# A hybrid decoder layer: weights of twelve projection units split early and kept in DRAM as two parts

## The chip, the cores and the metric

The kernel runs on one core of one Trainium2 chip. Its time is the device time of one execution in microseconds (us). TensorE (PE) does the matmuls, VectorE (DVE), ScalarE (ACT) and GpSimd (POOL) the rest, and SyncE (SP) issues nearly all DMAs. Each engine works through its own queue in order; semaphores order the engines among each other.

## What is computed

One layer over x of 1024 positions by 1024 columns. The reference, cut to what matters here:

```python
u = rms_norm(h, attn_norm[layer])
proj = jnp.einsum('bsd,dc->bsc', u, w_in[layer])
(dq, dk, dv, sq, ckv, iq, ik, iw, rq, rk, rv, gate) = jnp.split(proj, split_points, axis=-1)
o_a = diff_attention(dq, dk, dv, ...)            # two softmaxes a head, their difference times v
o_b = dsa_attention(sq, rms_norm(ckv), iq, ik, iw, ...)  # index scores, top 256 keys a query, attention
o_c = retention(rotary(rq), rotary(rk), rv, ...)
y = jax.nn.silu(gate) * concat(o_a, o_b, o_c)
h = h + jnp.einsum('bsc,cd->bsd', y, w_out[layer])
return rms_norm(h, final_norm)
```

## The kernel before

**Units.** The input projection is cut into units of 128 columns (256 for rq, rk, rv): iq0 to iq3 make the index queries, q0 to q2 and k0 to k2 the queries and keys of the differential attention, s0 to s2 and ck those of the sparse attention, g0 to g7 the gate. `gemm` runs a unit. Every product of two float32 operands is made of three matmuls over two-part numbers: uh and ul are the parts of u, wh and wl those of a weight. In the trace lines 130, 131 and 132 are the products wh x uh, wh x ul and wl x uh of a 128-column unit, and lines 347 to 349 those of a 256-column unit.

**The split.** `wsplit` loads a unit's weights in two halves of 256 KB into wr (two buffers, SP issues), and for each half POOL writes wh (L119, a rounding copy, 128x512) and wl (L123, the rest, 128x512). wh and wl live in tag w, five buffers of 4 KB a partition, so that two units fit and one tile of a third: wl of a unit can be written when the unit before the last one has ended on PE.

**Order.** `run` writes the program in stages: the front (v, index keys), iq0, iq1; then the index scores (`idx_scores`, lines 408 and 409 on PE, 411 on ACT, 416 on DVE) interleaved with iq2, iq3, q0, k0; then the differential attention (`diff`: scores L718, softmax L729 on DVE and L731 on ACT, POOL's scaling pq at L744, the combination L747 on DVE, transposes L678, product with v L693) beside the top-k bisection (`topk`, L443 to L464 on DVE, L457 on ACT, with one copy hb, L431, on POOL) and the remaining units; then the sparse attention, retention and the output. PE's queue has exactly the order in which the program is written. On the other engines a scheduler decides when the program is built: it takes, by its own estimate of time, whatever is ready and comes first in the program.

**Around the split.** POOL also splits some evicted results (hl, L119 and L366), rotates (rt), and finishes norms (f, L510 to L531). `mix` interleaves several streams by their costs and weights.

Of the kernel before, what the change touches and what calls it, by code (L numbers as in the profile page):

```python
# [10 lines left out]
F = mybir.dt.float32  # L11
FR = mybir.dt.float32r
# [9 lines left out]
KC = 8  # L22
# [5 lines left out]
C_DQ, C_DK, C_DV, C_SQ, C_CKV, C_IQ, C_IK, C_RQ, C_RK, C_RV, C_G = (  # L28
    0, 384, 768, 1152, 1536, 1664, 2176, 2248, 2504, 2760, 3016)
WA = 384 + 72  # L30
C_R = (C_RQ, C_RK, C_RV)
K = {'mk': 'up ky', 'mp': 's2 g5 g4', 'rt': ('hl', 'pq'), 's0': ('gg', 'ag', 'gg', 'ag', 'gg', 'ag', 'gg', 'ag'), 'xp': 2, 'bufs': (8, 3, 3, 5, 3, 4, 1), 'pp': (7,), 'rot': 0, 'order': 'g0 g1 k1 q1 k2', 'order2': 'q2 g2 rq g6 s0 ck g7 s1 M g3 rv rk | ', 'wd': 36, 'wt': 13, 'wg': 119, 'gw': 56, 'rw': 26, 'rx': 132, 'pw': 40, 'ow': 84, 'nf': 2, 'ev': 200, 'late': 8, 'de': ('aa', 'aa', 'aa'), 'da': 'ax', 'gd': (7, 4, 2), 'hlp': 'sqkk', 'tkp': '', 'vt': 'v', 'rs': 'x', 'nv': 1, 'dn': 'v', 'ws': 'gg', 'oe': ('av', 'gg'), 'one': 0, 'idx': (42, 40), 'iqs': 'iq2 iq3 q0 k0'}
NST, NP, NPQ, NW, NHL, NHALF, NY = K["bufs"]


# [10 lines left out]
def mix(*streams):  # L46
    live = [[g, float(total), 0.0] for g, total in streams]
    while live:
        s = min(live, key=lambda v: v[2] / v[1])
        try:  # L50
            c = next(s[0])
            s[2] += c
            yield c
        except StopIteration:
            live.remove(s)


def interleave(*streams):
    for _ in mix(*streams):
        pass  # L60


def drain(*gens):
    for g in gens:
        for _ in g:
            pass


class Trunk:
    def __init__(self, ctx, tc, ins, out):  # L70
        self.tc, self.nc = tc, tc.nc
        self.i, self.out = ins, out
        self.sb = ctx.enter_context(tc.tile_pool(name="sb", bufs=1))
        self.ps = ctx.enter_context(tc.tile_pool(name="ps", bufs=1, space=PSUM))
        self.dr = ctx.enter_context(tc.tile_pool(name="dr", bufs=1, space=bass.MemoryType.DRAM))
        self.n = 0
        self.late = []
        self.qd, self.gd, self.rt = {}, {}, {}
        self.yo = {c: self.dram(f"yo{c}", [128, S]) for c in (0, 1, 2)}
        self.gr = self.dram("gr", [2, 128, S])  # L80
        self.gd[6], self.gd[7] = self.gr[0], self.gr[1]
        self.yd = [self.dram(f"yd{j}", [8, 128, 512]) for j in range(2)]
# [225 lines left out]
    def wsplit(self, c0, w):  # L308
        hs, ls = [], []
        if w == WA:  # L310
            big = [self.sb.tile([128, 4, w], FR, name=self.name("wb"), tag="pt", bufs=2) for _ in range(2)]
            big += [self.sb.tile([128, 2, w], FR, name=self.name("wb"), tag="hl", bufs=NHL) for _ in range(2)]
            big += [self.wtile("wb", [2, w]) for _ in range(2)]
            hs = [big[k // 4][:, k % 4] for k in range(KC)]
            ls = [big[2 + k // 2][:, k % 2] for k in range(KC)]
            self.split_w = lambda k: self.split(hs[k], ls[k], self.dvw[k // 2][:, k % 2], *K["s0"][k])
            return hs, ls
        n = 1024 // w
        for k0 in range(0, KC, n):
            h, l = (self.wtile("w" + x, [n, w]) for x in "hl")  # L320
            for j in range(0, n, n // 2):
                raw = self.rtile([n // 2, w])
                self.nc.sync.dma_start(raw, self.i["w_in"][0, (k0 + j) * 128:(k0 + j + n // 2) * 128,
                                                           c0:c0 + w].rearrange("(k p) c -> p k c", p=128))
                self.split(h[:, j:j + n // 2], l[:, j:j + n // 2], raw, *K["ws"])
            hs += [h[:, j] for j in range(n)]
            ls += [l[:, j] for j in range(n)]
        return hs, ls

    def evict(self, evac, *args):  # L330
        with self.tc.high_priority(offset=K["ev"]):
            evac(*args)
# [21 lines left out]
    def to_dram(self, key, n=2):  # L354
# [543 lines left out]
    def run(self):  # L898
        nc = self.nc
        self.setup()  # L900

        def unit(t):
            x, n = t[0], t[1:]
            if t == "M":
                g = mix((units(K["mk"]), 8.2), (units(K["mp"]), 10.2 * len(K["mp"].split())))
            elif t == "ck":
                g = self.gemm(("b", C_CKV, 128, self.lazy2(self.ckv_evac)))
            elif t == "ky":
                g = self.kv_keys()
            elif t == "up":  # L910
                g = self.kv_up()
            elif t[:2] == "iq":
                g = self.gemm(("b", C_IQ + 128 * int(t[2]), 128, self.to_dram(t)))
            elif x == "r":
                g = self.gemm(("a", C_R["qkv".index(n)], 256, self.ret_evac(n)))
            elif x == "g":
                g = self.gemm(("b", C_G + 128 * int(n), 128, self.gate_evac(int(n))))
            else:
                c, key, m = {"q": (C_DQ, "dq", 4), "k": (C_DK, "dk", 4), "s": (C_SQ, "sq", 2)}[x]
                g = self.gemm(("b", c + 128 * int(n), 128, self.to_dram(key + n, m)))  # L920
            yield from g

        def seq(*gs):
            for g in gs:
                yield from g

        def units(s):
            return seq(*(unit(t) for t in s.split()))

        et = mybir.EngineType  # L930
        with self.tc.manual_schedule(engines={et.PE, et.DVE, et.SP}):
            keys = self.front()
        with self.tc.manual_schedule(engines={et.PE}):
            drain(units("iq0"))
            keys()
            drain(units("iq1"))
            interleave((seq(*(self.idx_scores(t) for t in range(4))), K["idx"][0]), (units(K["iqs"]), K["idx"][1]))
        self.setup_late()
        interleave((seq(*(self.diff(p) for p in range(3))), K["wd"]),
                   (seq(self.topk(), self.ties((3, 2))), K["wt"]),  # L940
                   (units(K["order"] + " " + K["order2"].split("|")[0]), K["wg"]))
        self.v_load()
        interleave((seq(*(self.dsa(p, 0) for p in range(3))), 100), (self.ties((7, 6, 5, 4)), 110),
                   (seq(units(K["order2"].split("|")[1]), mix((self.retention(0), K["rw"]),
                                (seq(self.out_weights(), self.project(K["pp"], 0)), K["ow"]))), K["gw"]))
        interleave((seq(*(self.dsa(p, 1) for p in range(3))), 100),
                   (mix((self.retention(1), K["rx"]), (self.project(range(K["nf"])), 100)), K["pw"]))
        drain(self.project(range(K["nf"], 3)))
        with self.tc.issue_after(self.last.ins):
            drain(self.project([3]))  # L950
        drain(self.project(range(NB - 1, 3, -1)))
# [100 lines left out]
```

## Time and profile before

| | us |
|---|---|
| median of 3 runs | 768.53 (767.16 to 770.72) |
| the profiled execution | 772.95 |
| its span, first to last instruction | 771.2 |
| PE busy | 718.2 (93%) |
| DVE busy | 559.9 (73%) |
| ACT busy | 458.6 (59%) |
| POOL busy | 310.4 (40%) |
| POOL: 56 wl, 56 wh | 79.9 and 40.3 |

The profile is one execution. An engine's busy share is an average over stages that differ, so a table of stretches says more than the totals. "Idle before" names what an engine waited for. The granted clock (PEclk) is the share of full speed that PE was allowed.

### The profile page before, as it was taken

What the parts mean: (1) busy time and instruction counts of PE and PEld (TensorE: products, weight loads), DVE (VectorE), ACT (ScalarE), POOL (GpSimd) and SP (SyncE); (2) the same over time, 40 slices, a digit from 0 to 9 for tenths busy, and PEclk for the clock granted to TensorE, in tenths of its full rate; (3) what the DMA queues carried; (4) which work ended last, traced back from release to release, by engine and by line L of the source; (5) the groups of instructions that cost most, each with busy time, mean ns of one, the idle gap of its engine ahead of it and who ended that gap; (6) DMA issues with size and microseconds to landing.
All of it is one profiled execution on the core that took longest, in us unless ns stands there. A gap on an engine that the chain in (4) does not pass through costs nothing.

```text
span 771.2 us, 12824 instructions
## 1 busy us (share of the span) xinstructions
PE 718.2 (93%) x4266; PEld 591.1 (77%) x4266; DVE 559.9 (73%) x1315; ACT 458.6 (59%) x1002; POOL 310.4 (40%) x343
## 2 busy tenths in 40 slices
PE   6999999999989999978889889999978999999996
PEld 5986788887878988756767668989756887777884
DVE  3684577989999989999889986426657775654443
ACT  4762555489687877786845655533355665653332
POOL 6422122434424539447347787337633332120000
PEclk9999999999999999999899989999979999999998
DMA  9716455472484344451383685565579964413441
GB/s 337 255 28 178 137 159 142 111 191 79 118 202 109 99 132 113 114 144 31 91 239 108 172 229 167 145 203 165 177 212 272 251 203 113 132 34 106 137 166 55
DMA packets 93618, 116.73 MB, mean 151 GB/s; under 512 B 11120, under 2 KB 62704, under 8 KB 93424
## 3 DMA queue, kind: packets, MB, share of 16 engines
q1 hardware_dynamic: 91152, 111.94, 50.8%
q10 hardware_dynamic: 2400, 3.97, 1.4%
q8 instruction: 34, 0.56, 0.3%
q14 instruction: 32, 0.26, 0.1%
HBM read 79.17 MB, written 36.18 MB: 150 GB/s over the span
## 4 chain that ended last, share of the span: by engine, by line
PE 62%; DVE 13%; DMA 8%; issue 7%; ACT 4%; POOL 4%; SPq 2%; ACTq 0%; DVEq 0%; POOLq 0%
PE pG L130 6%; PE pG L131 6%; PE pG L132 6%; PE pB L693 5%; PE pB L678 4%; PE pG L1003 4%; PE pG L1004 4%; PE pG L1005 4%; PE pS L272 3%; PE pG L347 2%; DVE jv L443 2%; PE pG L349 2%; PE pG L348 2%; PE pS L409 2%; PE pS L408 2%
## 5 line engine op out<-in xcount | busy, mean ns | idle before, releaser
L130 PE MATMUL pG<-uh,wh 128*128 128x512 f32 x352 | 142.5, 405 | 4.5 <-DVE gt L894 2.1
L132 PE MATMUL pG<-uh,wl 128*128 128x512 f32 x352 | 141.2, 401 | 1.7 <-POOL wl L123 1.7
L131 PE MATMUL pG<-ul,wh 128*128 128x512 f32 x352 | 140.4, 399 | 1.3 <-DVE ul L255 1.3
L123 POOL TENSOR_TENSOR wl<-wr,wh 128x512 fp32r<-128x512 f32 x56 | 79.9, 1443 | 84.4 <-PE pG L131 73.8
L457 ACT ACTIVATE ja<-sc,tk_c 128x896 int8<-128x896 f32 (+2 forms) x93 | 83.3, 896 | 22.3 <-DVE tk_c L464 16.5
L113 ACT ACTIVATE pt<-pB 128x512 f32<-128x512 f32 (+2 forms) x120 | 58.9, 496 | 41.9 <-PE pB L678 41.7
L130 PEld LDWEIGHTS pG<-uh,wh 128*128 128x128 f32 x352 | 67.5, 192 | 19.3 <-DVE gt L894 2.4
L132 PEld LDWEIGHTS pG<-uh,wl 128*128 128x128 f32 x352 | 67.4, 192 | 16.7 <-POOL wl L123 2.5
L131 PEld LDWEIGHTS pG<-ul,wh 128*128 128x128 f32 x352 | 67.4, 191 | 15.5 <-DVE ul L255 3.3
L678 PE MATMUL pB<-ident,pp 128*128 128x128 f32 x432 | 73.4, 288 | 4.6 <-DVE gt L825 1.9
L693 PE MATMUL pB<-pt,v 128*64 128x128 f32 x864 | 68.0, 294 | 7.4 <-ACT pt L113 6.8
L693 PEld LDWEIGHTS pB<-pt,v 128*64 128x64 f32 x864 | 55.3, 143 | 18.9 <-ACT pt L113 9.5
L443 DVE TENSOR_SCALAR_CACHE_REDUCE jv<-sc,tk_c 128x640 bf16<-128x640 f32 (+4 forms) x81 | 69.1, 853 | 0.9
L119 POOL TENSOR_SCALAR wh<-wr 128x512 fp32r<-128x512 f32 x56 | 40.3, 723 | 69.9 <-DMA wr<-in_w_in_dram 50.8
L678 PEld LDWEIGHTS pB<-ident,pp 128*128 128x128 f32 x432 | 51.7, 145 | 20.4 <-issue 8.5
L744 POOL TENSOR_SCALAR pq<-pq,mx 128x896 f32<-128x896 f32 (+7 forms) x48 | 39.2, 816 | 58.5 <-DVE mx L743 46.1
L347 PE MATMUL pG<-wh,uh 128*128 128x256 f32 x192 | 55.4, 290 | 0.7 <-POOL wh L119 0.7
L411 ACT ACTIVATE pp<-pS 128x1024 f32<-128x1024 f32 (+5 forms) x48 | 36.5, 760 | 31.5 <-PE pS L409 31.5
L348 PE MATMUL pG<-wl,uh 128*128 128x256 f32 x192 | 55.0, 287 | 0.0
L349 PE MATMUL pG<-wh,ul 128*128 128x256 f32 x192 | 54.4, 284 | 0.0
L747 DVE SCALAR_TENSOR_TENSOR pp<-pp,mx,pq 128x896 f32<-128x896 f32 (+7 forms) x48 | 51.1, 1065 | 4.4 <-POOL pq L744 3.6
L416 DVE SCALAR_TENSOR_TENSOR sc<-pp,iw,sc 128x1024 f32<-128x1024 f32 (+5 forms) x42 | 43.5, 1048 | 14.6 <-ACT pp L411 14.2
(234 smaller groups left out, 1731.4 us busy)
## 6 DMA issues: line engine op xcount, KB each, us to landing
wr<-in_w_in_dram SPq DMA_DIRECT2D x56, 256.0 KB, 3.1
st<-qdq SPq DMA_DIRECT2D x24, 256.0 KB, 4.2
st<-qkk SPq DMA_DIRECT2D x18, 256.0 KB, 6.1
qiq<-hl SPq DMA_DIRECT2D x16, 256.0 KB, 3.5
st<-qiq SPq DMA_DIRECT2D x8, 512.0 KB, 3.4
wr<-in_w_out_dram SPq DMA_DIRECT2D x16, 256.0 KB, 3.3
xr<-in_x_dram SPq DMA_DIRECT2D x8, 512.0 KB, 3.6
yr<-yd SPq DMA_DIRECT2D x7, 512.0 KB, 4.1
```

The source lines that it names most:

```text
L113: self.nc.scalar.activation(out, in_, AF.Copy)
L123: (self.nc.vector if e2 == "v" else self.nc.gpsimd).tensor_tensor(lo, src, hi.bitcast(F), OP.subtract)
L130: mm(ps, wh, xh, start=start, stop=False)
L131: mm(ps, wh, xl, start=False, stop=False)
L132: mm(ps, wl, xh, start=False, stop=stop)
L347: mm(ps, uh, hs[k], start=k == 0, stop=False)
L348: mm(ps, uh, ls[k], start=False, stop=False)
L349: mm(ps, ul, hs[k], start=False, stop=k == KC - 1)
L443: nc.vector.tensor_scalar(jv[:, :nv[b]], hb if b == 7 and bit >= 16 else sc[b], t, 0.0, op0=op, op1=OP.add, accum_out=cnt[:, j:j + 1])
L457: nc.scalar.activation(ja[:, :nv[b]], sc[b], AF.Sign, bias=cut(b), scale=-1.0, accum_out=cnt[:, cols[b]:cols[b] + 1])
L678: nc.tensor.transpose(p[:, k], pr[:, (k0 + k) * 128:(k0 + k + 1) * 128], self.ident)
L693: self.last = nc.tensor.matmul(o[u * 64:(u + 1) * 64], vals[k], pts[g, a][:, k, u * 128:(u + 1) * 128], start=k == (i if u else 0), stop=k ...
```

## The change

Twelve weight tiles of 1024 columns a partition are handled differently: those of q2, g2, rq (two tiles), g6, s0, ck, g7, s1, s2, g5 and g4. A new stream `presplit` stands as a third one beside the index scores. For each tile it loads the raw weights (512 KB, wp, a buffer of tag w), and for each of its two halves POOL writes ph and pl into half-size buffers (tag h, four buffers) and POOL itself issues two stores, of ph and of pl, to a DRAM tensor ws. `wsplit` then loads wh and wl of these units from ws, 512 KB each, with SP and without POOL. The units g0, g1, k1, q1, k2, g3, rv and rk and those of the index scores are split as before. The table K gains two entries: `ps`, the list of units, and `pz`, 1.0.

```diff
@@ __init__
+        self.ws = {}
@@ wsplit
             h, l = (self.wtile("w" + x, [n, w]) for x in "hl")
-            for j in range(0, n, n // 2):
+            if c0 in self.ws:
+                for x, t in enumerate((h, l)):
+                    self.nc.sync.dma_start(t.bitcast(F), self.ws[c0][k0 // n][:, x])
+            for j in range(0, n if c0 not in self.ws else 0, n // 2):
                 raw = self.rtile([n // 2, w])
...
+    def presplit(self, cols):
+        for c0, w in cols:
+            n = 1024 // w
+            d = self.ws[c0] = self.dram(f"ws{c0}", [w // 128, 128, 2, n, w])
+            for k0 in range(0, KC, n):
+                raw = self.wtile("wp", [n, w], F)
+                self.nc.sync.dma_start(raw, self.i["w_in"][0, k0 * 128:(k0 + n) * 128,
+                                                           c0:c0 + w].rearrange("(k p) c -> p k c", p=128))
+                for j in range(0, n, n // 2):
+                    src = raw[:, j:j + n // 2]
+                    hi, lo = (self.half(x, (128, n // 2, w), FR) for x in ("ph", "pl"))
+                    self.split(hi, lo, src, "g", "g")
+                    for x, t in enumerate((hi, lo)):
+                        self.nc.gpsimd.dma_start(d[k0 // n][:, x, j:j + n // 2], t.bitcast(F))
+                    yield 1.0
@@ run (seq_cols turns the names of ps into columns and widths)
-            interleave((seq(*(self.idx_scores(t) for t in range(4))), K["idx"][0]), (units(K["iqs"]), K["idx"][1]))
+            interleave((seq(*(self.idx_scores(t) for t in range(4))), K["idx"][0]), (units(K["iqs"]), K["idx"][1]),
+                       (self.presplit(seq_cols(K["ps"])), 2.0 * len(K["ps"].split()) * K["pz"]))
```

POOL's queue before, in the stage of the index scores (numbers are those of buffers): the four operations of iq3 (wh_841, wl_842), then of q0 (wh_1012, wl_1013):

```order
L119 TENSOR_SCALAR wh_841<-wr_843 128x512
L119 TENSOR_SCALAR wh_841<-wr_847 128x512
L123 TENSOR_TENSOR wl_842<-wr_843,wh_841 128x512
L123 TENSOR_TENSOR wl_842<-wr_847,wh_841 128x512
L119 TENSOR_SCALAR wh_1012<-wr_1014 128x512
L119 TENSOR_SCALAR wh_1012<-wr_1018 128x512
L123 TENSOR_TENSOR wl_1013<-wr_1014,wh_1012 128x512
L123 TENSOR_TENSOR wl_1013<-wr_1018,wh_1012 128x512
```

One unit's operations follow directly on the last one's. In the changed order (its lines 120 and 124 are the old 119 and 123; 347 is the new store), POOL's queue at the split of q0, wh_1101 and wl_1102:

```order
L120 TENSOR_SCALAR wh_1101<-wr_1107 128x512
L120 TENSOR_SCALAR ph_981<-wp_979 128x512
L124 TENSOR_TENSOR pl_982<-wp_979,ph_981 128x512
L347 DMA ws_978<-ph_981 128x512
L120 TENSOR_SCALAR ph_1018<-wp_979 128x512
L347 DMA ws_978<-pl_982 128x512
L124 TENSOR_TENSOR pl_1019<-wp_979,ph_1018 128x512
L347 DMA ws_978<-ph_1018 128x512
L120 TENSOR_SCALAR ph_1050<-wp_1048 128x512
L347 DMA ws_978<-pl_1019 128x512
L124 TENSOR_TENSOR wl_1102<-wr_1103,wh_1101 128x512
L124 TENSOR_TENSOR wl_1102<-wr_1107,wh_1101 128x512
```

Between wh and wl of the unit stand two and a half halves of another unit's weights with four stores; between the wl of iq3 and this wl there are 28 rows in all, of which four are q0's own. The copy hb of the top-k stood before g1's wl in POOL's queue:

```order
L119 TENSOR_SCALAR wh_1491<-wr_1493 128x512
L119 TENSOR_SCALAR wh_1491<-wr_1497 128x512
L431 TENSOR_SCALAR hb<-sc_662 128x1024
L123 TENSOR_TENSOR wl_1492<-wr_1493,wh_1491 128x512
L123 TENSOR_TENSOR wl_1492<-wr_1497,wh_1491 128x512
```

In the changed order the whole split of g0 (wh_1578, wl_1579) comes after hb:

```order
L451 TENSOR_SCALAR hb<-sc_662 128x1024
L120 TENSOR_SCALAR ph_1367<-wp_1365 128x512
L347 DMA ws_1276<-pl_1330 128x512
L124 TENSOR_TENSOR pl_1368<-wp_1365,ph_1367 128x512
L347 DMA ws_1364<-ph_1367 128x512
L120 TENSOR_SCALAR ph_1399<-wp_1365 128x512
L347 DMA ws_1364<-pl_1368 128x512
L120 TENSOR_SCALAR wh_1578<-wr_1580 128x512
L120 TENSOR_SCALAR wh_1578<-wr_1584 128x512
L124 TENSOR_TENSOR pl_1400<-wp_1365,ph_1399 128x512
L347 DMA ws_1364<-ph_1399 128x512
L120 TENSOR_SCALAR ph_1443<-wp_1441 128x512
```

The two rows of wl_1579 follow on the last one. hb, which waits for the index scores of the last block, moved ahead of one more unit. PE's order of units and scores is the same in both; the scheduler's order on DVE, ACT and SP shifts by a few places.

## Rows read from the trace of the kernel before

**Rows 1.** Table of stretches: us, busy us (instructions) by engine, PEclk, DMA share, GB/s.

```profile
65.00:152.00 87.00, 86.25 (x404) 72.09 (x402) 57.37 (x70) 42.78 (x60) 24.95 (x21) 1.00 0.56 155
152.00:300.00 148.00, 144.01 (x854) 121.35 (x854) 138.72 (x381) 117.19 (x264) 65.42 (x79) 0.99 0.49 127
300.00:400.00 100.00, 85.86 (x486) 67.65 (x484) 91.87 (x236) 74.86 (x175) 53.57 (x58) 0.97 0.45 120
400.00:492.00 92.00, 84.58 (x467) 67.45 (x468) 77.29 (x166) 55.69 (x128) 68.68 (x63) 0.93 0.59 167
...
200.00:220.00 20.00, 18.04 (x95) 14.61 (x95) 18.73 (x59) 15.64 (x43) 5.20 (x6) 0.92 0.57 139
```

The five busy columns are PE, PEld (its weight loads), DVE, ACT and POOL.

**Rows 2.** Costliest groups, POOL: busy us, mean ns of one | idle before.

```profile
L123 POOL TENSOR_TENSOR wl<-wr,wh 128x512 fp32r<-128x512 f32 x56 | 79.9, 1443 | 84.4 <-PE pG L131 73.8
L119 POOL TENSOR_SCALAR wh<-wr 128x512 fp32r<-128x512 f32 x56 | 40.3, 723 | 69.9 <-DMA wr<-in_w_in_dram 50.8
L744 POOL TENSOR_SCALAR pq<-pq,mx 128x896 f32<-128x896 f32 (+7 forms) x48 | 39.2, 816 | 58.5 <-DVE mx L743 46.1
```

**Rows 3.** DMA issues on SP and ACT, ns min/median/max; landings of qiq.

```profile
L370 SPq DMA_DIRECT2D qiq<-hl x16: 580/598/1192, 58.9 to 119.6; - x16
...
DMA to landing us min/median/max: 3.1/3.5/6.4
...
L1020 ACTq DMA_DIRECT2D out_dram<-xr x8: 338/362/369, 670.2 to 767.3; - x8
```

**Rows 4.** The subtraction of a split, 512 columns, on POOL and on DVE.

```profile
L123 POOL TENSOR_TENSOR wl<-wr,wh x56: 1267/1294/3240, 31.2 to 523.8; 128x512 fp32r<-128x512 f32 x56
...
L123 DVE TENSOR_TENSOR hl<-pG,hl 128x512 fp32r<-128x512 f32 x10 | 6.9, 686 | 11.1 <-ACT hl L113 11.1
```

**Rows 5.** POOL in order of time: start us, us, instruction, idle before.

```profile
64.73 2.54 POOL L123 TENSOR_TENSOR wl<-wr,wh 128x512 fp32r<-128x512 f32 x2 [10.19 <-PE pG L131]
...
97.41 3.53 POOL L123 TENSOR_TENSOR wl<-wr,wh 128x512 fp32r<-128x512 f32 x2 [12.36 <-PE pG L131]
...
144.86 1.04 POOL L431 TENSOR_SCALAR hb<-sc 128x1024 bf16<-128x1024 bf16 x1
```

**Rows 6.** PE in order of time: first L132 of iq3, q0, k0, g0, g1.

```profile
97.78 0.39 PE L132 MATMUL pG<-uh,wl 128*128 128x512 f32 x1
...
117.36 0.40 PE L132 MATMUL pG<-uh,wl 128*128 128x512 f32 x1
...
136.84 0.39 PE L132 MATMUL pG<-uh,wl 128*128 128x512 f32 x1
...
153.19 0.39 PE L132 MATMUL pG<-uh,wl 128*128 128x512 f32 x1
...
164.47 0.40 PE L132 MATMUL pG<-uh,wl 128*128 128x512 f32 x1
```

**Rows 7.** DVE in order of time: L416 beside POOL's wl, and without.

```profile
97.91 1.88 DVE L416 SCALAR_TENSOR_TENSOR sc<-pp,iw,sc 128x1024 f32<-128x1024 f32 x1 [0.85 <-ACT pp L411]
...
107.29 1.28 DVE L416 SCALAR_TENSOR_TENSOR sc<-pp,iw,sc 128x1024 f32<-128x1024 f32 x1 [1.53 <-ACT pp L411]
```

**Rows 8.** Who waited for whom, PE, 300 to 492: us, times, longest.

```profile
PE pB L693 <- ACT pt L113: 6.3, 2, 3.5
PE pS L718 <- DVE mx L729: 4.3, 7, 0.9
PE pS L718 <- DMA qsq<-hl: 2.5, 1, 2.5
PE pG L130 <- ACT hl L364: 2.0, 2, 1.2
PE pG L132 <- POOL wl L123: 1.7, 2, 1.1
PE pG L130 <- DVE gt L894: 1.4, 1, 1.4
PE pB L678 <- DVE yo L115: 1.1, 1, 1.1
```

More of the change, by code (lines that the diff above doesn't have):

```diff
@@ L31 @@
 C_R = (C_RQ, C_RK, C_RV)
-K = {'mk': 'up ky', 'mp': 's2 g5 g4', 'rt': ('hl', 'pq'), 's0': ('gg', 'ag', 'gg', 'ag', 'gg', 'ag', 'gg', 'ag'), 'xp': 2, 'bufs': (8, 3, 3, 5, 3, 4, 1), 'pp': (7,), 'rot': 0, 'order': 'g0 g1 k1 q1 k2', 'order2': 'q2 g2 rq g6 s0 ck g7 s1 M g3 rv rk | ', 'wd': 36, 'wt': 13, 'wg': 119, 'gw': 56, 'rw': 26, 'rx': 132, 'pw': 40, 'ow': 84, 'nf': 2, 'ev': 200, 'late': 8, 'de': ('aa', 'aa', 'aa'), 'da': 'ax', 'gd': (7, 4, 2), 'hlp': 'sqkk', 'tkp': '', 'vt': 'v', 'rs': 'x', 'nv': 1, 'dn': 'v', 'ws': 'gg', 'oe': ('av', 'gg'), 'one': 0, 'idx': (42, 40), 'iqs': 'iq2 iq3 q0 k0'}
+K = {'mk': 'up ky', 'mp': 's2 g5 g4', 'rt': ('hl', 'pq'), 's0': ('gg', 'ag', 'gg', 'ag', 'gg', 'ag', 'gg', 'ag'), 'xp': 2, 'bufs': (8, 3, 3, 5, 3, 4, 1), 'pp': (7,), 'rot': 0, 'order': 'g0 g1 k1 q1 k2', 'order2': 'q2 g2 rq g6 s0 ck g7 s1 M g3 rv rk | ', 'wd': 36, 'wt': 13, 'wg': 119, 'gw': 56, 'rw': 26, 'rx': 132, 'pw': 40, 'ow': 84, 'nf': 2, 'ev': 200, 'late': 8, 'de': ('aa', 'aa', 'aa'), 'da': 'ax', 'gd': (7, 4, 2), 'hlp': 'sqkk', 'tkp': '', 'vt': 'v', 'rs': 'x', 'nv': 1, 'dn': 'v', 'ws': 'gg', 'oe': ('av', 'gg'), 'one': 0, 'idx': (42, 40), 'iqs': 'iq2 iq3 q0 k0', 'ps': 'q2 g2 rq g6 s0 ck g7 s1 s2 g5 g4', 'pz': 1.0}
 NST, NP, NPQ, NW, NHL, NHALF, NY = K["bufs"]
@@ L925, in seq, with seq_cols @@
                 yield from g
+        def seq_cols(s):
+            at = {"q": C_DQ, "k": C_DK, "s": C_SQ, "g": C_G}
+            out = []
+            for t in s.split():
+                if t == "ck":
+                    out.append((C_CKV, 128))
+                elif t[0] == "r":
+                    out.append((C_R["qkv".index(t[1])], 256))
+                else:
+                    out.append((at[t[0]] + 128 * int(t[1]), 128))
+            return out
         def units(s):
```

## The prediction

> **What bounds the kernel now.** I read the page's busy times first, TensorE (PE) far ahead of the others, and since an average hides four stages, then the table of stretches, one row for each [rows 1]. From 65 to 152 us (index scores beside the projection units iq2, iq3, q0, k0) PE is busy 86.25 of 87 us at full clock: nothing can be gained there, and whatever makes PE wait is lost in full. From 152 to 300 us (differential attention, top-k and the units g0, g1, k1, q1, k2, q2, ...) it is nearly as full, 144.0 of 148. Only from 300 to 492 us does PE stand idle: 14.1 + 7.4 = 21.5 us, and the granted clock is 0.97 and 0.93 there, which is another 100 x 0.03 + 92 x 0.07 = 9.4 us. POOL is busy 53.6 of 100 and 68.7 of 92 us there, VectorE (DVE) 91.9 and 77.3. So the change takes work from POOL where it is fullest and PE waits, and puts it where POOL is emptiest (25 of 87 us) but PE has no slack.
>
> **What the split costs.** A unit's weights are two 512-column halves; for each, POOL makes wh (mean 723 ns) and wl (mean 1443 ns) [rows 2]: 2.17 us, means that hold the usual delays from other engines. Twelve 1024-column tiles are 24 halves, 24 x 2.17 = 52 us of POOL, half of it taken from 196 to 300 us (q2, g2, rq's two tiles, g6, s0) and half from 300 to 450 (ck, g7, s1, s2, g5, g4). The change adds the same 52 us as ph and pl beside the index scores, and 48 stores that POOL itself issues, two for each half. The 24 raw loads become 12 of double size in the early stage, and 24 loads of 512 KB (wh and wl) stand where the raw ones were.
>
> **Price of a store on POOL: the disputed number.** No row shows POOL issuing a DMA. The nearest rows: ACT, which also computes between its issues, takes 0.36 us for one, SP 0.60 us for the store of a split tile, and such a store lands 3.5 us after its issue [rows 3]. The low end is 0.36. The high end is POOL held until the store has landed, 3.5. POOL is the slower engine for the same work: a 512-column subtraction takes it 1294 ns where DVE needs 686 [rows 4], 1.88 times. I take SP's 0.60 us times 1.88 = 1.13 us, since SP's row is the one for this very transfer shape (both halves of a split tile to DRAM).
>
> The Trainium skill, "DMA: Bandwidth & Descriptors", section Specifications, gives about 1 us to the first byte for a DMA issued by GpSimd and 0.6 us for one by SP or ACT. If that whole microsecond were POOL's own, the ledger below would come to 19 us in place of 25 and the result to 781; no run here shows it yet.
>
> **The ledger of POOL's queue.** POOL runs in order, and the order is fixed when the program is built. In the changed order the wl of a unit stands behind several halves of presplit work. Who waits for it is PE: the unit's first L132 matmul needs it, and all of PE's queue, index scores too, stands behind that matmul. Before, wl of q0 ran at 97.41 us [rows 5], when q0's first L132 came at 117.36 [rows 6]: 16 us of slack. The units iq3, q0, k0, g0, g1 need wl at 97.8, 117.4, 136.8, 153.2 and 164.5 [rows 6]. The presplit starts after iq2's wl (64.73 + 2.54 us [rows 5]), when its first 512 KB have come: about 69. Between one unit's wl and the next the new order has, as (0.723 us operations, 1.443 us operations, stores), the unit's own four operations included:
> to iq3: 7, 6, 8 = 13.7 + 9.0 = 22.8 us, ready at 91.8, in time;
> to q0: 8, 8, 12 = 17.3 + 13.6 = 30.9, ready at 122.6, 5.2 late;
> to k0: 7, 7, 9 = 15.2 + 10.2 = 25.3, ready at 148.0, needed at 136.8 + 5.2: 5.9 late;
> to g0: 7, 7, 10 and hb (1.04 [rows 5]) = 27.5, at 175.5, needed at 153.2 + 11.1: 11.2 late;
> to g1: 4, 4, 5 and one pq (0.8 [rows 2]) = 15.1, at 190.6, needed at 164.5 + 22.3: 3.8 late;
> to k1: in time, and with it the presplit ends.
> Sum: 26 us, less 1.4 since PE's first L132 needs only the first of the two wl: 25. A unit's period on PE is 19.5 us, and POOL now needs 25 to 31 for the same stretch. At 0.36 us for a store the same ledger has only g0 late, by 2.5 us: hb waits for the index scores (144.86 [rows 5]) and g0's split now stands behind it.
>
> PE pays for such waits in clock too. In 200 to 220 us PE idled 2.0 us and the clock of the stretch was 0.92, 1.6 us of work lost [rows 1]. Four waits like it: 6 us. This part runs at PE's limit, so I count it in full, between 0 and 11 (the 9.4 us lost for 21.5 idle, times 25).
>
> **What lies beside it.** DVE: L416 took 1.88 us beside POOL's wl and 1.28 us without it for the same 1024 columns [rows 7], so each of 48 new POOL operations may hold up one L416 by 0.6 us, 29 us at most. DVE is busy 57.4 of 87 us and the ledger stretches this stage and the next by 25, so PE does not feel it: 0. DMA: the early stage runs at a share of 0.56 and 155 GB/s; 12 tiles of 0.5 MB in and 24 halves of 0.5 MB out add 19 MB, 68 us at 277 GB/s (155/0.56), against 0.44 x 87 = 38 us free before 152 and as much after. It fits, tightly. If stores land in 6.4 us (the slowest [rows 3]) rather than 3.5, the ph of the next half but one waits for its buffer: 1 us on each of 22 halves. I take 0 and keep 20 for the upper end. SP: each weight load now waits for PE to release a buffer of tag w, where it waited for POOL before; behind it on SP stand the st loads of the next attention head, and PE's L718 waits for those. From 300 to 492 the longest such wait is 2.5 us [rows 8]; I take 0, with 5 in the upper end.
>
> **What is gained from 300 to 492 us.** POOL loses 6 x 4.33 = 26 of its 122 busy us there. PE's waits for wl (1.7 us) and for hl of L364, evicted through POOL's queue (2.0), go [rows 8]: 3.7. Its waits for ACT's pt (6.3), for DVE's mx (4.3), gt and yo (2.5) go back to a DVE that is itself full, and that POOL's operations lengthen; I take a third of 13.1: 4.4, for POOL keeps four fifths of its work. Clock in proportion, 9.4 x 8.1 / 21.5 = 3.5. Sum 11.6, say 12. What is late next is DVE, which stays nearly full. Lower end: 3.7, if DVE's own work keeps all its waits. Upper: 20. From 196 to 300 us the relief buys nothing, since PE hardly waits there.
>
> **Sum.** 25 + 6 - 12 = +19 us. The profiled execution took 772.95 us, 771.2 of it in the span, and is 4.4 us above the median of the three runs, 768.53. I put the sum on the median: 787.5, as 787.
>
> **Rivals.**
> *The issue is cheap.* POOL only hands the store over, as ACT does, in 0.36 us. Then the backlog is 2.5 us and the relief stays 12: 768.5 - 9.5 = 759; with the relief's upper end, 20, below 756. For it: the issues of ACT and SP lie near 0.36 and 0.60 [rows 3]. Against: POOL's software is slower in every row where it can be compared. This is also how a rule of the Trainium skill would have it ("DMA: Bandwidth & Descriptors", section Issuing engines are not separate DMA queues): a DMA's initiation is usually small beside the DMA itself. The ledger's 26 becomes 11.5 at 0.8 us a store and 7 at 0.7; gain and loss balance near 0.75. Chance 0.25.
> *It balances.* A store of 0.65 to 0.8 us: 765 to 772. Chance 0.10.
> *My forecast*, a store of 0.9 to 1.3 us with relief later: 773 to 798. Chance 0.50.
> *Relief that does not reach the path.* The backlog is as forecast, but from 300 to 492 us DVE stays the bound (91.9 of 100 us busy) and only the 3.7 us go: 768.5 + 25 + 6 - 4 = 796, and up to 808 with half of the late stores and of SP's waits. This is where it turns out slowest. Chance 0.12. A POOL that is held until stores land goes beyond: at 3.5 us each the ledger gives some 130 us. Chance 0.03.
>
> **How the numbers follow.** The likeliest is 787. The range takes in the cheap issue, from 756, and the relief that does not reach the path, to 808. Within 0.5% of before (764.7 to 772.4) is about what a measurement here can't tell from no change: 0.10. Faster 0.25, slower 0.65. The forecast's own range is 773 to 798.
>
> **What would show it.** In the new profile: POOL full from 70 to about 200 us, with PE's idle time in that stretch put down to POOL's wl, at the starts of q0, k0, g0, g1; POOL's issues of the ws stores near 1.1 us, by the spacing of its neighbours; PE's first L130 of k1 some 30 us later than 179. Later, L747 shorter, no wait of PE for wl between 300 and 492, and less idle time there. I would be wrong if POOL's stores leave no gap between its operations, if the index scores stage still ends by 153, or if PE's waits between 300 and 492 stay above 20 us.

## The result, and the profile after

The changed kernel takes **812.08 us** (802.64 to 813.23, five runs) against 768.53: a ratio of **1.052** with a 95% interval of 1.048 to 1.056, slower by 43.5 us. It lies 25 us above the forecast of 787 and 4 us above the end of the range, 808. The profiled execution is the fastest of the five (802.64, span 800.9). A second series, h0 below, gave a ratio of 1.050 (1.046 to 1.055) and a profile near the median, span 811.9; both profiles are read here.

Tables of stretches, as in [rows 1]: us, busy us (instructions) of PE, PEld, DVE, ACT and POOL, then PEclk, DMA share, GB/s. The kernel before, in the stretches that compare best:

```profile
65.00:110.00 45.00, 44.25 (x207) 36.70 (x205) 23.64 (x28) 19.99 (x29) 12.71 (x12) 1.00 0.60 171
110.00:152.00 42.00, 42.00 (x198) 35.39 (x197) 33.74 (x43) 22.80 (x32) 12.24 (x9) 1.00 0.51 138
152.00:200.00 48.00, 46.94 (x238) 38.58 (x238) 45.39 (x117) 38.31 (x81) 20.15 (x20) 1.00 0.49 129
200.00:300.00 100.00, 97.06 (x617) 82.78 (x617) 93.33 (x265) 78.88 (x185) 45.27 (x59) 0.98 0.48 125
300.00:500.00 200.00, 178.44 (x1028) 142.79 (x1027) 171.33 (x410) 133.74 (x311) 122.91 (x121) 0.95 0.52 144
```

The changed kernel, first profile:

```profile
65.00:110.00 45.00, 42.21 (x193) 34.54 (x192) 27.36 (x26) 18.65 (x27) 30.42 (x37) 1.00 0.91 281
110.00:152.00 42.00, 38.02 (x164) 30.94 (x163) 38.78 (x28) 19.31 (x27) 39.33 (x43) 0.92 0.89 275
152.00:200.00 48.00, 34.75 (x128) 26.08 (x127) 46.41 (x89) 26.59 (x52) 36.15 (x44) 0.82 0.75 222
200.00:300.00 100.00, 98.41 (x603) 82.46 (x602) 94.21 (x276) 84.50 (x199) 25.39 (x34) 1.00 0.58 166
300.00:500.00 200.00, 174.22 (x973) 138.06 (x971) 166.47 (x419) 128.47 (x296) 85.96 (x94) 0.94 0.52 151
```

The changed kernel, second profile (h0):

```profile
65.00:110.00 45.00, 42.01 (x192) 34.40 (x191) 28.21 (x26) 18.54 (x27) 30.79 (x37) 1.00 0.94 289
110.00:152.00 42.00, 35.49 (x152) 28.91 (x151) 39.16 (x27) 17.77 (x26) 37.46 (x44) 0.92 0.94 277
152.00:200.00 48.00, 30.70 (x117) 23.85 (x115) 44.95 (x71) 22.46 (x42) 30.61 (x37) 0.82 0.66 188
200.00:300.00 100.00, 98.24 (x559) 81.06 (x559) 93.91 (x270) 84.40 (x194) 27.30 (x35) 0.97 0.55 160
300.00:500.00 200.00, 174.61 (x1000) 138.91 (x997) 170.04 (x434) 130.22 (x301) 86.07 (x97) 0.93 0.54 154
```

A way to read them: PE's busy time multiplied by its clock is the work that it got done in a stretch. The clock has two digits, so a cell is good to about 1 us, and to 2 in the longest stretch.

| PE work done, us at full clock | 65 to 200 | 200 to 300 | 300 to 500 | sum of differences | span longer by |
|---|---|---|---|---|---|
| before | 133.2 | 95.1 | 169.5 | | |
| after, first profile | 105.7 (-27.5) | 98.4 (+3.3) | 163.8 (-5.7) | -29.9 | 29.7 |
| after, second profile | 99.8 (-33.4) | 95.3 (+0.2) | 162.4 (-7.1) | -40.3 | 40.7 |

So the loss is 27 to 33 us beside the index scores and just behind them. The later columns have to be read with care: a kernel that is 30 us late does other work from 300 to 500 us than the kernel before did. Two readings allow for that. The first is when the same instruction starts; the first matmul of k1, before, in the first and in the second profile:

```profile
178.97 0.47 PE L130 MATMUL pG<-uh,wh 128*128 128x512 f32 x1 [0.67 <-DVE gt L894]
208.45 0.39 PE L131 MATMUL pG<-uh,wh 128*128 128x512 f32 x1
216.40 0.40 PE L131 MATMUL pG<-uh,wh 128*128 128x512 f32 x1
```

It is 29.5 and 37.4 us late, and the span is 29.7 and 40.7 us longer: from k1 to the end another 0.2 and 3.3 us are lost. The second reading takes the last stretch 30 us later in the first profile, and 38 in the second:

```profile
330.00:530.00 200.00, 176.60 (x1008) 140.21 (x1007) 147.67 (x379) 121.04 (x286) 84.55 (x90) 0.94 0.53 153
338.00:538.00 200.00, 175.93 (x997) 138.80 (x997) 146.84 (x377) 119.22 (x283) 84.17 (x89) 0.93 0.53 152
```

That is 166.0 and 163.6 us of work, 3.5 and 5.9 less than before. By either reading the forecast's gain of 12 isn't there, though POOL is busy 84 to 85 us in that stretch instead of 123.

Who waited for whom, PE, 65 to 202 us (us in all, times, longest). First profile:

```profile
PE pS L738 <- DVE mx L749: 6.3, 3, 3.4
PE pG L133 <- POOL wl L124: 5.4, 3, 2.8
PE pG L131 <- POOL wh L120: 4.3, 1, 4.3
PE pS L428 <- DMA st<-qiq: 1.7, 3, 1.3
...
PE pG L131 <- DVE hl L124: 0.2, 1, 0.2
```

Second profile:

```profile
PE pG L131 <- DVE hl L124: 10.4, 1, 10.4
PE pG L133 <- POOL wl L124: 6.0, 2, 3.8
PE pS L738 <- DVE mx L749: 2.9, 2, 2.6
...
PE pG L131 <- POOL wh L120: 1.6, 1, 1.6
```

(Lines 131 to 133 are the old 130 to 132, L428 the old 408, L436 the old 416, L738 the old 718.) The waits for POOL's wl and wh stand at q0, k0 and g0, but they are only 8 to 10 us of the 20 to 27 that PE idled. One wait divides the two profiles: g0's second column block, which needs the PSUM bank that DVE's hl frees, waited 0.2 us in one and 10.4 in the other, about the distance between them.

### The profile page after: what moved, and what is told of

Its sections match the earlier page's. It is cut to its first block, busy times and chain, and to the rows that moved or that the text cites. A ratio compares the mean times of both kernels' runs of the same rounds, so it can differ in the third digit from the quotient of the medians.

```text
span 800.9 us, 12944 instructions
## 1 busy us (share of the span) xinstructions
PE 725.2 (91%) x4266; PEld 592.7 (74%) x4266; DVE 573.9 (72%) x1315; ACT 457.4 (57%) x1002; POOL 329.4 (41%) x391
## 4 chain that ended last, share of the span: by engine, by line
PE 49%; DVE 16%; DMA 14%; POOL 7%; ACT 6%; issue 5%; SPq 1%; DVEq 0%; ACTq 0%; POOLq 0%
PE pB L713 4%; PE pG L131 4%; PE pG L133 4%; PE pG L132 4%; PE pB L698 4%; PE pG L1036 4%; PE pG L1037 4%; PE pG L1038 3%; ACT ja L477 3%; DMA wl<-ws 3%; PE pS L273 3%; DVE jv L463 2%; POOL pl L124 2%; PE pG L368 2%; PE pG L369 2%
## 5 line engine op out<-in xcount | busy, mean ns | idle before, releaser
L131 PE MATMUL pG<-uh,wh 128*128 128x512 f32 x352 | 146.1, 415 | 12.5 <-DMA wh<-ws 5.2
L133 PE MATMUL pG<-uh,wl 128*128 128x512 f32 x352 | 142.4, 405 | 11.1 <-DMA wl<-ws 5.6
L132 PE MATMUL pG<-ul,wh 128*128 128x512 f32 x352 | 143.2, 407 | 0.8 <-DVE ul L256 0.8
L131 PEld LDWEIGHTS pG<-uh,wh 128*128 128x128 f32 x352 | 69.1, 196 | 29.1 <-DMA wh<-ws 5.6
L132 PEld LDWEIGHTS pG<-ul,wh 128*128 128x128 f32 x352 | 68.9, 196 | 15.2 <-DVE ul L256 2.4
L713 PE MATMUL pB<-pt,v 128*64 128x128 f32 x864 | 64.2, 284 | 5.5 <-ACT pt L114 4.8
L436 DVE SCALAR_TENSOR_TENSOR sc<-pp,iw,sc 128x1024 f32<-128x1024 f32 (+5 forms) x42 | 62.0, 1513 | 7.3 <-ACT pp L431 7.0
L713 PEld LDWEIGHTS pB<-pt,v 128*64 128x64 f32 x864 | 52.1, 137 | 17.4 <-ACT pt L114 8.2
L738 PE MATMUL pS<-st,st 128*128 128x512 f32 (+3 forms) x144 | 45.2, 381 | 14.4 <-DVE mx L749 9.6
L749 DVE CUSTOM_DVE_ANT_0 pp<-pS,cb 128x896 f32<-128x896 f32 (+7 forms) x48 | 36.0, 750 | 30.4 <-PE pS L738 17.4
L124 POOL TENSOR_TENSOR wl<-wr,wh 128x512 fp32r<-128x512 f32 x32 | 42.9, 1355 | 26.8 <-PE pG L132 16.0
```

Source lines behind the costliest of these rows:

```text
L124: (self.nc.vector if e2 == "v" else self.nc.gpsimd).tensor_tensor(lo, src, hi.bitcast(F), OP.subtract)
L131: mm(ps, wh, xh, start=start, stop=False)
L132: mm(ps, wh, xl, start=False, stop=False)
L133: mm(ps, wl, xh, start=False, stop=stop)
L436: nc.vector.scalar_tensor_tensor(acc, rel, iw, acc, op0=OP.mult, op1=OP.add)
L713: self.last = nc.tensor.matmul(o[u * 64:(u + 1) * 64], vals[k], pts[g, a][:, k, u * 128:(u + 1) * 128], start=k == (i if u else 0), stop=k ...
```

## Experiments: which part costs what

Each ratio is against the kernel before, run beside it on the same chip (medians 770 to 772); a per cent is 7.7 us.

**e1_loads_alone**: the later part alone.

```diff
-                       (self.presplit(seq_cols(K["ps"])), 2.0 * len(K["ps"].split()) * K["pz"]))
+                       (self.presplit(seq_cols("q2")), 2.0))
+            for c0, w in seq_cols(K["ps"]):
+                self.ws[c0] = [self.ws[C_DQ + 256][0]...] * 2      # viewed as [128, 2, n, w]
```

> Of the presplit only its first tile is left (two halves, four stores); every later unit of the list loads two 512 KB parts from that one tile's place in DRAM, so the loads keep their number, size and shape, and the weights' values are not the units' own. This is the later part of the change alone. Theory: the relief of POOL after 200 us is eaten by PE's new waits for these loads (wl from ws 5.6 us, wh 5.2 us, 10.8 in all between 300 and 520 us in the changed kernel), so the time stays between 765 and 775 us. Rival, the forecast's own relief of 12 us, with the changed kernel's extra loss lying in the early part: 754 to 760 us.

Measured: 778.34, ratio 1.010 (1.007 to 1.013), 3 us above the theory's range. POOL is rid of its splits almost for nothing, and the kernel is slower. PE's waits from 300 to 500 us, where [rows 8] had pt 6.3, mx 4.3, qsq 2.5, hl 2.0, wl 1.7:

```profile
PE pS L738 <- DMA st<-qdk: 8.4, 3, 4.0
PE pG L133 <- DMA wl<-ws: 4.9, 2, 3.5
PE pS L738 <- DVE mx L749: 4.7, 6, 1.2
PE pS L738 <- DMA st<-qdq: 2.9, 1, 2.9
```

The waits for pt, hl and POOL's wl have all but gone; waits for loads stand in their place.

**e2_early_alone**: the presplit without its use.

```diff
-            d = self.ws[c0] = self.dram(f"ws{c0}", ...)
+            d = self.dram(f"ws{c0}", ...)
```

> The presplit and its 48 stores stay, but the units load and split their weights themselves, as in the kernel before. This is the early part alone. Theory: it costs all that the change costs, 30 us where k1 begins (about 208 us, against 179.0), and nothing is given or taken later: 800 to 813 us. Rival (the later part gives back 12 us, as forecast): 824 us, since then the early part must cost 43.5 + 12.

Measured: 803.80, ratio 1.042 (1.034 to 1.050), 32 us. With e1's 8 that makes 40, the whole loss: within e2's interval (26 to 38 us) the two parts add, and the later one gives nothing back.

**g4_loads_only, e3_no_stores, e4_no_split**: the early part step by step. g4 makes nothing of the raw tiles but the first (`for j in ... if c0 == C_DQ + 256 else ()`); e3 splits all and stores the first alone (`... (hi, lo) if c0 == C_DQ + 256 else ()`); e4 stores the raw half twice in place of ph and pl:

```diff
-                    hi, lo = (self.half(x, ...) for x in ("ph", "pl"))
-                    self.split(hi, lo, src, "g", "g")
-                    for x, t in enumerate((hi, lo)):
-                        self.nc.gpsimd.dma_start(d[k0 // n][:, x, j:j + n // 2], t.bitcast(F))
+                    for x in (0, 1):
+                        self.nc.gpsimd.dma_start(d[k0 // n][:, x, j:j + n // 2], src)
```

> The presplit splits all twelve tiles, but only the first tile's four stores are left, and later loads read that tile's place (values not the units' own). POOL saves 44 issues of about 0.58 us = 26 us, and 11.5 MB are not written. Theory A, POOL's queue is what PE waits for: k1 begins 5 to 12 us later than before instead of 29.5, 785 to 795 us. Theory B, the loads of raw tiles come late because the DMA engines are nearly full (share 0.91 from 65 to 110 us): share falls to about 0.65 and the result is the same, 785 to 795; this run with the next one tells them apart. Theory C, the buffers of tag w that the raw tiles take, and SP's order: hardly less than the changed kernel, 805 to 812 us.

> The raw halves are stored twice each, so that loads and stores are those of the changed kernel, but POOL splits nothing early: 24 x (0.62 + 1.3) = 46 us less on POOL (values of the weights' parts are wrong by that). Theory A, POOL's queue: k1 begins within 5 us of before, and the time is 775 to 785 us. Theory B, the DMA engines are full: k1 still begins 20 us late or more, 800 us or more. Theory C, buffers and SP's order: also 800 us or more.

> The twelve raw tiles are loaded early as in the changed kernel, but only the first is split and stored; later loads read that place (values not the units' own). With e1 (no early loads, 778 us) and e4 (loads and stores without splits, 788) it gives the price of the loads on SP and in the buffers of tag w. Theory (POOL's time is what counts): 778 to 782. Rival (a good part of the early loss is the loads, which hold the buffers and SP): 785 us or more.

Measured:

| kernel | contains | us | ratio (95%) | us over before |
|---|---|---|---|---|
| e1 | later loads | 778.34 | 1.010 (1.007 to 1.013) | 8 |
| g4 | and early raw loads | 786.80 | 1.021 (1.018 to 1.025) | 16 |
| e4 | and stores, no splits | 787.81 | 1.022 (1.017 to 1.027) | 17 |
| e3 | early loads and splits, no stores | 801.19 | 1.039 (1.034 to 1.043) | 30 |
| after (h0) | all | 810.59 | 1.050 (1.046 to 1.055) | 39 |

e3 fell between the ranges of its theories, and e4 lies 3 us above that of theory A. Later loads (with one tile's presplit) 8, early loads 8, splits 14, stores 9. These are steps in one order: in the other, from g4 over e4 to the whole, the stores cost 1 and the splits 22, so that neither has a price of its own. The stores' traffic is nearly free: without splits they cost 1 us, at a DMA share of 0.93 and 1.00 (e4, 65 to 110 and 110 to 152 us). In g4 the loads' price is nearly one wait, of 65 to 202 us:

```profile
PE pS L430 <- DMA st<-qiq: 6.0, 1, 6.0
```

Beside it stands the granted clock, 0.85 from 65 to 110 us; e1 has 1.00 there, and 3.2 us of this wait.

In e3 PE waits for st too, at 14.0 us in all, and SP's waits in the same stretch say why:

```profile
SPq L327 <- POOL wl L124: 41.3, 12, 9.0
SPq L340 <- POOL pl L124: 16.1, 5, 5.9
```

SP stands still for POOL before loads of wr (L327) and wp (L340), and the st loads that the index scores need stand behind these in its queue. A late POOL so reaches PE by a second way, through SP. In the whole change this way is a small one, 2.6 and 2.3 us of waits for st, so that the 14 us which the splits cost in e3 are not lost in the same place.

**e7_sp_stores, f3_split_act_dve, g2_pool_free, h3_pool_free_later**: the whole change, with POOL relieved. e7: `self.nc.gpsimd.dma_start` of the stores becomes `self.nc.sync.dma_start`. f3: `self.split(hi, lo, src, "g", "g")` becomes `self.split(hi, lo, src, "a", "v")`. g2: both. h3: g2 with a `yield 8.0` ahead of the first load, and 8 more in the stream's cost.

> The changed kernel in full, with the 48 stores issued by SP instead of POOL: POOL is free of 48 x 0.58 = 28 us, the traffic is the same. e3, without the stores, was 11 us faster than the changed kernel. Theory A (POOL's issuing time is what the stores cost): about 800 us. Theory B (the stores' traffic costs it): 812, no change. Theory C (SP's queue, on which the stores now wait for POOL with the st and wr loads behind them): above 815.

> The changed kernel in full, but the early split makes ph on ACT and pl on DVE; POOL only issues the stores. ACT takes about 24 x 0.5 = 12 us and DVE 24 x 0.69 = 17 us of it; both are busy about half of 65 to 110 us, DVE nearly full from 152 us. Theory A (time that POOL's queue is occupied is what the early part costs, since e4 without the 46 us of splits was 24 us faster): the same gain but for what DVE's longer queue takes back, 788 to 800 us. Rival (work on any engine of this stage delays PE as much, DVE's most, as index scores wait for it): 805 us or more.

> The changed kernel in full with both edits at once: ph on ACT and pl on DVE, and the stores issued by SP, so that POOL does nothing for the presplit. Alone, they took off 13.6 and 13.3 us. Theory (POOL's time is the price, and the two parts of it add): 812 - 27 = 785, between 780 and 790. Rival (both removed the same wait, at the same units): 796 to 800.

> The changed kernel in full with ph on ACT, pl on DVE, the stores on SP and the presplit put off by a quarter of the stage: what is left of the cost when POOL does none of it and the first burst is avoided. If both add to g2's 793: 783 to 787. Even so it can't come below the 778 of the later loads alone. Rival (squeezed into less time, its loads and stores delay st and wr elsewhere): 792 or more.

Measured: e7 798.79 (1.034; 1.031 to 1.036), f3 798.43 (1.034; 1.030 to 1.038), g2 792.87 (1.028; 1.024 to 1.032), h3 794.54 (1.032; 1.029 to 1.036). Issuing on SP saves as much as leaving the stores out did, so of the stores it is POOL's time that counts. Splitting on ACT and DVE saves 12 to 13 us of what e4 saved by not splitting (23); those engines take the rest. The two edits together save 18 to 19, not 27, perhaps because they shorten partly the same waits. A later start doesn't help.

**i1_issues_for_split**: POOL's queue without work on data. To e4, for each half:

```diff
+                    for _ in range(4):
+                        self.nt += 1
+                        self.nc.gpsimd.dma_start(self.tiny[self.nt][:, 0:w], raw[0:32, j])
```

> The kernel of e4_no_split (raw halves stored twice, no early split; 788 us), with four further small stores by POOL for each half (32 rows of 512 or 1024 bytes): 96 issues of about 0.55 us = 53 us of POOL's time, a little more than the 46 us of splits that e4 left out, and 2 MB of traffic, but no work of POOL on data. Queue theory (the splits cost what they hold up in POOL's queue): wl and wh are late again, 805 to 815 us. Port theory (they cost what they lengthen on VectorE): VectorE's index-score operations stay at 45 to 47 us, and the time within 5 us of e4, 785 to 793.

Measured: 832.58, ratio 1.081 (1.074 to 1.088), 45 us above e4, more than either theory said. What POOL issued, and PE's waits, 65 to 202 us:

```profile
L349 POOL DMA_DIRECT2D tiny<-wp x96: 496/502/685, 70.5 to 198.1; - x96
```

```profile
PE pG L131 <- POOL wh L120: 15.4, 1, 15.4
PE pS L740 <- DMA st<-qdk: 14.1, 2, 10.1
PE pS L430 <- DMA st<-qiq: 6.3, 2, 4.5
PE pG L133 <- POOL wl L124: 3.3, 2, 2.7
```

The 96 issues are 96 x 0.50 = 48 us, and POOL stood another 14 us before some of them for earlier stores. DVE's 42 index-score operations (L438 in this kernel) took 41.8 us, no longer than before. So time in POOL's queue is enough to cost PE what the splits cost, without any lengthening of DVE's work, and by both ways, POOL's own wh and wl and SP's st. The small stores are traffic too, so the 45 us are not a clean price of 48.

**The later part, why no relief: f1, f2, g1.** All three are e1 with another kind of later load: f1 issues them on POOL (`self.nc.gpsimd.dma_start`), f2 in halves of 256 KB, g1 only their first 128 columns (`t[:, 0:1]`, and PE uses that chunk throughout).

> The kernel of e1_loads_alone (only the first tile's presplit; weights not the units' own), with the 24 loads of wh and wl issued by POOL instead of SP. In e1 the old waits of PE between 300 and 500 us for ACT's pt and hl, POOL's wl and yo had gone (about 11 us), but its waits for loads had grown from 6.3 to 17 us (st 11.7, wl 5.3). Theory: these loads stand in SP's queue behind waiting stores, and st loads behind them; on POOL, idle half of that stretch, they are out of SP's way: 760 to 768 us. Rival 1, a load of 512 KB that can start only when its buffer is free is late by its landing time (5.4 us) from whatever queue: 775 to 782, as e1. Rival 2, POOL now stands still for the buffers and holds up pq and hl: above 782.

> The kernel of e1_loads_alone, with each 512 KB load of wh and wl made as two loads of 256 KB on SP, first halves of both first, so that a unit can begin when its first half has landed. Theory (SP's queue order): hardly another time, 774 to 782 us, since as many loads stand behind the same waiting stores and SP issues 24 more of 0.35 us. Rival, the size of the load is what makes wl late: PE's 5.3 us of waits for wl go, 768 to 774.

> The kernel of e1_loads_alone with each later load of wh or wl cut to its first 128 columns, 64 KB for 512 KB; PE uses that chunk for all eight (weights wrong by that). Number, order and waits of the loads stay; their traffic and landing time are an eighth and perhaps two thirds. e1 took 778 us, the kernel before 771 beside it. Theory (POOL's relief is not on the path of 300 to 500 us; the waits of PE only change their names): 770 to 780, POOL at 32 and 54 of 100 us in the two stretches and PE idle there still 20 us. Rival (the relief is real, 12 us, and only the transfers' landing takes it back): 758 to 765.

Measured: f1 784.98 (1.017; 1.014 to 1.020), f2 777.49 (1.008; 1.005 to 1.010), g1 768.88 (0.998; 0.995 to 1.000). My theory for f1 fell: POOL now stands still for buffers, and PE waited 11.1 us for mx (190 to 510 us). f2, as its theory had it, says that loads of half the size are no help. g1 settles it: with loads of an eighth the 8 us go, and no gain comes. PE's waits in g1, 300 to 500 us:

```profile
PE pS L738 <- DVE mx L749: 6.7, 6, 2.6
PE pB L713 <- ACT pt L114: 4.0, 3, 1.8
PE pB L698 <- ACT yo L116: 1.9, 1, 1.9
```

These are names of [rows 8] (yo is DVE's there), at 12.6 us beside 11.7 for the three there, though POOL does 29 us less in this stretch (93.84 busy, not 122.91). Read as above (busy time by clock), g1's PE gets 2.6 us more done than before from 200 to 300 us and 1.5 us more from 300 to 500; it has 4.4 less before 200, mostly one wait of 3.6 us for st beside the one tile that e1 and g1 still split early. But h1 below, which has no relief at all, read in the same way has 3.6 us and 2.0 us more than the one profile of before (98.71 us busy at a clock of 1.00, and 178.63 at 0.96): the profiled execution of before lost 3.6 us between 200 and 220 us alone [rows 1]. So POOL's relief is worth at most some 4 us, a third of the forecast, when loads cost next to nothing, and none of it is shown; with real loads e1 is 9 us slower than g1.

**g3_three_tiles**: `'ps': 's2 g5 g4'`.

> The changed kernel with only s2, g5 and g4 split early: 3 tiles instead of 12, in the first stretch where POOL has room, their loads later where POOL is busiest (400 to 490 us). Theory (a loss that grows with POOL's added time once its room is used up; nothing is gained later): early 0 to 5 us, later 0 to 5 us, 769 to 780. Rival (relief of the fullest stretch is worth something when it costs nothing early): 760 to 766, faster than before.

Measured: 784.45, ratio 1.018 (1.015 to 1.021), 14 us and above both forecasts: a quarter of the tiles costs a third of the loss. No smaller share of this change is seen to pay.

**h0_after_again, h1_wd37, h2_loads_later**: the changed kernel again; the kernel before with `'wd': 37` for 36; and g4 with the delay of h3.

> The changed kernel itself, for a second profile and a closer median. Its five runs were 802.6 (the profiled one) and 811.5 to 813.2. If 812 is its time, the median stays at 808 to 813 and a profile near 810 shows where 8 us more are lost: early (PE's waits for POOL's wl and wh, 9.7 us in the first profile) by the theory that POOL's queue decides, or evenly by a lower granted clock. If the first runs were disturbed, the median comes to 802 to 805.

> The kernel before with one weight of the interleaving (wd, the differential attention's share) 37 for 36: the same instructions, but PE's queue in another order in 532 of its rows, the other engines' too. Theory (order alone is worth a few microseconds, so differences of that size between these kernels are not to be read as work): 766 to 778. If it stays within 2 us of before, order matters little and e1's 8 us are work; above 778, order is a cause of the first rank.

> The kernel of g4_loads_only (raw tiles loaded, only the first split and stored), with the start of these loads put off by a quarter of the stage, so that the first comes behind iq3's weights. Theory (the 9 us of the early loads are the burst from 66 to 95 us, in which st comes late): 777 to 781, as e1, and no wait of PE for st above 3 us. Rival (the loads cost by the buffers of tag w and SP's queue wherever they stand): 785 to 790.

Measured: h0 810.59 (802.32 to 815.52); h1 769.36, ratio 0.999 (0.997 to 1.002); h2 788.20, ratio 1.021 (1.015 to 1.027). In this one case another order alone costs nothing. In h2 the rival held: the early loads cost 8 us wherever they start, so the burst of transfers before 95 us isn't their cause. Two of the loads start before 95 us in h2 and at least five in g4, and PE's longest wait for st is 2.4 us instead of 6.0, at the same total. Buffers and SP's queue remain, and which of the two is open.

## Why the prediction was wrong, and where it was right

**The sign and the early loss were right: 31 us forecast (25 of waits, 6 of clock), 27.5 and 33.4 lost by 200 us.** The first L131 of k1 came 29.5 and 37.4 us later than before (some 30 forecast), POOL was full (39 of 42 us from 110 to 152), and PE's clock fell to 0.92 and 0.82 behind its waits, which lost 38.02 x 0.08 + 34.75 x 0.18 = 9 us in the first profile (6 forecast). The way there was right in part: 8 to 10 us of PE's waits were for POOL's wl and wh, where 25 were forecast.

**But the disputed price was wrong by two, and the early sum held by luck.** A store keeps POOL 0.56 to 0.59 us, not 1.13:

```profile
L347 POOL DMA_DIRECT2D ws<-ph x24: 557/558/760, 70.3 to 198.7; - x24
L347 POOL DMA_DIRECT2D ws<-pl x24: 539/587/598, 71.7 to 202.6; - x24
```

It is SP's 0.60 [rows 3]; scaling it by 1.88 from an arithmetic operation was the error. The Trainium skill, "DMA: Bandwidth & Descriptors", section Issuing engines are not separate DMA queues, has an initiation as usually small beside the DMA; here 0.58 us beside a median landing of 4.5 to 5.2 agrees. It doesn't follow that issues are cheap: 48 of them ahead of other work cost 9 us. With 0.58 in it, the prediction's ledger would have given some 4 us of backlog, an estimate by its own rows. What it left out made up for that, first POOL's own waits, here of the first profile, 65 to 205 us:

```profile
POOL ph L120 <- DMA wp<-in_w_in_dram: 11.3, 3, 5.4
...
POOL ph L120 <- DMA ws<-ph: 4.4, 5, 1.6
POOL pl L124 <- DMA ws<-pl: 1.2, 2, 1.0
```

The presplit waited 17 us for its raw tiles and for its stores to land, and in an order fixed beforehand every wl behind it waited along. So the rival "the issue is cheap" (0.36 us) was nearer in the price and wrong in the end.

**DMA and SP, taken as 0, were 8 us.** g4 measured the early loads; the prediction had them under "fits, tightly", with 20 kept for the upper end.

**DVE, taken as 0 of at most 29, was not free.** The 42 operations of L416, now L436 (busy us, mean ns), in the kernel before, in h0, and in e4, where POOL splits nothing early:

```profile
L416 DVE SCALAR_TENSOR_TENSOR sc<-pp,iw,sc 128x1024 f32<-128x1024 f32 (+5 forms) x42 | 43.5, 1048 | 14.6 <-ACT pp L411 14.2
```

```profile
L436 DVE SCALAR_TENSOR_TENSOR sc<-pp,iw,sc 128x1024 f32<-128x1024 f32 (+5 forms) x42 | 69.0, 1688 | 8.2 <-ACT pp L431 8.0
```

```profile
L434 DVE SCALAR_TENSOR_TENSOR sc<-pp,iw,sc 128x1024 f32<-128x1024 f32 (+5 forms) x42 | 43.1, 1039 | 18.6 <-ACT pp L429 18.4
```

They grew by 18.5 us in the first profile (62.0) and 25.5 in the second. The premise "DVE is busy 57 of 87 us" didn't last: from 110 to 152 us it is now busy 39 of 42. DVE also frees PSUM for PE, and in h0's order of time the last scores hold up hl, for which PE waited those 10.4 us:

```profile
165.30 3.33 DVE L436 SCALAR_TENSOR_TENSOR sc<-pp,iw,sc 128x512 f32<-128x512 f32 x1
168.56 3.87 DVE L438 TENSOR_TENSOR sc<-sc,cb 128x128 f32<-128x128 f32 x1
...
176.75 0.69 DVE L124 TENSOR_TENSOR hl<-pG,hl 128x512 fp32r<-128x512 f32 x1
```

How much of the splits' 14 to 22 us is this, and how much POOL's queue, the runs don't separate: i1 shows that the queue suffices, not that it is all.

**The step that failed is the gain from 300 to 492 us: 12 us forecast, a loss of 0 to 8 measured.** From k1 to the end the two profiles lose 0.2 and 3.3 us, and e1, the later part by itself, is 8 us slower than before. By the medians the change costs 43.5 us and not 19; of these 24.5, the 12 not gained and e1's 8 are 20. Two terms were wrong. *Relief:* the waits named there did shrink, but e1 and g1 show the time going to the next wait, and g1, with next to nothing to load, gains at most 4 us of 12. DVE did become freer, as hoped: from 300 to 500 us it was busy 171 us before, 159 in e1 and 161 in g1, and the 48 operations of its L747 fell from 1065 ns in the mean to 961 and 912. But PE went on waiting there for mx, pt and yo, which come from DVE and ACT, and its idle time rose from 21.6 us to 23.4 and 24.1 in the matching stretches. That these waits form a chain, from PE's scores through DVE and ACT and back, is read from their names; no run tests it. One row was misread, too: hl of L364 is ACT's copy [rows 8], which POOL only splits afterwards. *Loads:* the prediction had a term for the st loads behind the weight loads ("I take 0, with 5 in the upper end"; PE's waits for them were 2.6 and 3.3 us) and none for PE's own wait for the weight loads, which measured 9 to 11 us. PE's waits, first profile, 300 to 500 us:

```profile
PE pG L133 <- DMA wl<-ws: 5.6, 2, 3.6
PE pG L131 <- DMA wh<-ws: 5.2, 1, 5.2
PE pS L738 <- DVE mx L749: 3.4, 5, 1.8
PE pB L713 <- ACT pt L114: 3.3, 2, 2.8
PE pS L738 <- DMA st<-qdk: 2.6, 3, 1.7
```

Before, the raw halves and wh mostly stood ready when PE gave a buffer of tag w free (POOL's idle time before wl was for PE, 73.8 of 84.4 us [rows 2]), and wl followed at 1.3 us a half [rows 4]. Now the transfer itself starts only then, behind whatever SP is waiting for, and lands 5.3 to 5.8 us after its issue (medians of wl and wh). The change put a load on the path in place of a computation that was ready beside it.

**The rivals.** "Relief that does not reach the path" (796 to 808, chance 0.12) comes nearest to what happened; it was given too little chance, and 812 lies outside it, since it too had no term for PE's wait for the weight loads. Its reason, a DVE that stays the bound, isn't borne out: in e1 and g1 DVE became freer, and PE gained little or nothing. POOL was not held until stores land (0.58 us, not 3.5).

**One statement on the order was too strong.** The part ahead of the prediction says that PE's queue is that of the program. This holds for the units and the index scores; the attention's first scores moved: L738 now comes after 38 of the units' matmuls that follow the last index score, where it came after 63, and eight of them stand in one row, with PE's waits for DVE's mx (6.3 and 2.9 us) there. No run takes this order by itself; h1 shows only that one other order costs nothing.

## What to carry to other kernels

Work that is taken off an engine which isn't the bound is worth what a run without it shows, and that can be measured first: leave the work out (e1, g1), and if the time doesn't fall, no cheap place for it will help. Before a computation is replaced by a load, ask when each can start: the load waits for its buffer and for its queue, the computation may have had its input beside it. On an engine with a fixed order, what it waits for counts as much as what it does.

## What was not expected of the hardware

- A DVE operation with two inputs in SBUF can be held far longer than it takes: L438, 128x128, took 3.87 us at 168.56 us of the second profile, against 0.28 at 173.89, while POOL ran one operation behind the other. The 42 index-score operations show what it goes with: in the profiles where POOL splits all twelve tiles early (both of the changed kernel, e2, e3, e7) they took 1377 to 1688 ns in the mean, and where it splits none early (before, e4, f3, g2, i1) 1004 to 1084, with its stores or without. The Trainium skill, "SBUF — State Buffer", section SBUF: two separate sides, tells of a port that DVE's operations with two SBUF inputs and POOL's hold for a whole instruction, the other one waiting; the rows agree with that, but a delay of 3.6 us is more than one of POOL's operations there (1.3 us), which no run explains.
- POOL issues a store of 256 KB in 0.56 to 0.59 us and one of 16 to 32 KB in 0.50: the issue hardly depends on the size.
- Executions of one program differ by some 10 us: the two profiles of the changed kernel by 11 (800.9 and 811.9), where one wait, 0.2 and 10.4 us, is the largest difference between the traces, and the 17 of the kernel before that ran beside h0 by 10 (766.0 to 775.9).
